# Nine groups of small DMA transfers moved from SyncE's queue to GpSimd's in a fused decoder trunk

## The chip, the cores and the metric

One core of one Trainium2 chip runs the whole program in one launch. The metric is device microseconds (us) of one execution. Lower is better.

Engine names are those of the profile: PE is TensorE (matmul), PEld its weight loads, DVE is VectorE, ACT is ScalarE, POOL is GpSimd, SP is SyncE, which in this kernel only issues transfers. SPq is SP's issuing of a transfer. In the trace each engine works through its own list in the order in which the program wrote it, and idle time ahead of one instruction delays all that stand behind it on that engine.

## What is computed

Two layers of a decoder trunk on 256 tokens of width 1024. A layer is a feed-forward block, a mixing block and a second feed-forward block. The mixing block projects the tokens once and hands the columns to three groups of heads: a depthwise causal convolution of 31 taps, an attention, and a gated DeltaNet. The DeltaNet part is what the change touches. For each of 6 heads and 4 chunks of 64 tokens it needs the inverse of a unit lower triangular matrix:

```python
L = jnp.where(strict, jnp.einsum('bhncd,bhnsd->bhncs', k_beta, k) * decay, 0.0)
eye = jnp.eye(C, dtype=F32)
T = lax.linalg.triangular_solve(eye + L, jnp.broadcast_to(eye, L.shape), left_side=True, lower=True)
u = T @ v_beta
w = T @ (k_beta * jnp.exp(g)[..., None])
```

## The kernel before

The weights come from DRAM in pieces of up to 1 MB into four buffers named `raw`, all issued by SP. ACT rounds each piece to a high part `hi`, DVE makes the rest `lo`, and PE multiplies with three products (hi by hi, hi by lo, lo by hi). A piece's buffer is free again when its last reader is done, and only then may SP issue the next piece into it.

The order of the work on each engine is set while the program is written: a `Clock` object (class at L78, `note` at L133) keeps an estimated time for every engine, and `tick` (L1659) lets a dozen generators (`sides`) add their next instructions when the estimate says that their inputs are ready. All engine calls pass through one helper line, L171, so every row of the profile says L171 and is told apart by its tile's name.

The inverse runs in these steps:

1. `pairs` (L1257) writes the products of all heads into `LD` (a part of the tile shown as `xin_LT`), and four transfers (L1266) bring the 32x32 diagonal blocks to the DRAM tensor `scr_l`.
2. `inverse` (L1367) reads the 16x16 blocks back with two transfers (L1378) into `Lb`, 96 blocks on 96 partitions. POOL makes `Um`, a part of the same buffer, with four multiplications (L1382).
3. DVE does the substitution on all 96 blocks, 15 steps of a product into `T` and a subtraction from `W` (L1385 to L1391), and a copy that turns the result into `W[:, 1]` (L1392).
4. Four transfers (L1398) write `W` to `scr_w`, two for the plain inverse and two for the turned copy, and two transfers (L1400) read it back as 32x32 blocks into `Wc`.
5. POOL clears a tile (`S6a`), and PE joins the blocks to the 64x64 inverses, starting from `Wc` and `Lb`.

`scr_w` is cleared once, after the first feed-forward block: POOL sets a tile `E` to zero and two transfers (L1962) bring it to DRAM.

Beside the inverse runs the convolution of 31 taps (`taps`, L1522; `tap`, L1498). A tap is done in one of two ways: by one DVE instruction, or by a product on ACT into a tile `ctap` followed by an addition on POOL into `cacc` (L1509 and the two lines after it):

```python
m = sb([128, S], "ctap", bufs=2)
act.activation(m, hc[:, b, k:k + S], AF.Copy, scale=w)
gp.tensor_tensor(ca[:, b], ca[:, b], m, op=OP.add)
```

`ctap` has two buffers, so ACT's product number n can start only when POOL's addition number n - 2 is done. While the estimate has DVE busy with the substitution, the taps go this second way.

Also in this stretch PE works on the queries and keys of the attention (`rotary`, L1705): three pairs of projections, each into its own PSUM bank, which ACT copies out (`rope`, L1711; rows COPY Y<-pm), and then on the values (`mv`, L1837), which reuse the banks that these copies have freed.

Of the kernel before, what the change touches and what calls it, by code (L numbers as in the profile page):

```python
# [79 lines left out]
class Clock:  # L80


    def __init__(self):
        self.t = dict(pe=0.0, act=0.0, dve=0.0, gp=0.0, dma=0.0)
        self.writes, self.reads, self.used, self.slots, self.free = {}, {}, {}, {}, {}
        self.table = None
        self.filler = None
# [45 lines left out]
    def note(self, engine, op, args, kw):  # L133
        if op == "preload_act_table_set":
            self.t["act"] += 1.28 if args[0] != self.table else 0.0
            self.table = args[0]
            return
        out = kw.get("out", args[0] if args else None)
        ins = [x for x in list(args[0 if "out" in kw else 1:]) + [v for k, v in kw.items() if k not in ("out", "accum_out")]
               if hasattr(x, "tensor")]  # L140
        name = out.tensor.name
        start = max([self.t[engine], self.free.get(name, 0.0), self.last(self.reads, out), engine != "dma" and self.ready(out)]
                    + [self.ready(x) + 0.1 for x in ins])
        filler = self.filler
        if engine == "dve" and filler:
            self.filler = None
            while start - self.t["dve"] > HOLE and filler():
                pass
            self.filler = filler
            start = max(start, self.t["dve"])  # L150
        if engine == "dma":
            n = self.size(out) * out.shape[0] * 4 / 360e3
            self.t["dma"] = start + n
            end = start + n + (4.5 if "scr_" in name + ins[0].tensor.name else 2.0)
        else:
            end = self.t[engine] = start + self.cost(engine, op, out, ins)
        for log, aps in ((self.writes, [out, kw.get("accum_out", out)]), (self.reads, ins)):
            for x in aps:
                lo, hi = (0, 1 << 40) if engine == "dma" and x is out else self.span(x)
                w = log.setdefault(x.tensor.name, [])  # L160
                w[:] = [y for y in w if not (lo <= y[0] and y[1] <= hi)] + [(lo, hi, end)]
                self.used[x.tensor.name] = max(self.used.get(x.tensor.name, 0.0), end)
# [15 lines left out]
def trunk(ctx, tc, t, out):  # L178
    nc = tc.nc
# [1 line left out]
    psum = ctx.enter_context(tc.tile_pool(name="ps", bufs=1, space=PSUM))  # L181
    ctx.enter_context(tc.manual_schedule())
    clock = Clock()
    act, dve, pe, gp, sp = (clock.engine(n, e) for n, e in (("act", nc.scalar), ("dve", nc.vector), ("pe", nc.tensor),
                                                            ("gp", nc.gpsimd), ("dma", nc.sync)))

    def sb(shape, tag, dt=F32, bufs=1):
        return clock.tile(tag, bufs, pool.tile(shape, dt, name=tag, tag=tag, bufs=bufs))

    def ps(shape, tag, bufs=1):  # L190
        return clock.tile("p" + tag, bufs, psum.tile(shape, F32, name="p" + tag, tag="p" + tag, bufs=bufs))
# [64 lines left out]
    p = ps([128, 128], "x")  # L256
# [367 lines left out]
    def rstd(p=None):  # L624
        r = nscr["r"]
        if p is None:
            p = ps([128, S], "x")
            mm(p, ones, nscr["sq"][:, OB_ORDER[0]], True)
        act.activation(r, p, AF.Ln, bias=eps, scale=1.0 / D)
        act.activation(r, r, AF.Exp, scale=-0.5)  # L630
# [375 lines left out]
    scr_l = nc.dram_tensor("scr_l", [12, 4, 32, 32], F32, kind="Internal").ap()  # L1006
    scr_w = nc.dram_tensor("scr_w", [2, 12, 4, 32, 32], F32, kind="Internal").ap()
    late = {}

    def mixing(l, G, normed, nxt):  # L1010
# [47 lines left out]
        def until(*names):  # L1058
            while any(n not in ev for n in names):
                yield  # L1060
# [78 lines left out]
        LD = LT[:, :NH * 256].rearrange("p (h t x) -> p h t x", t=2, x=128)  # L1139
# [102 lines left out]
        def products(h, rhs):  # L1242
            b, r = half(h)
            yield from room()
            p = pside([128, 384], True)
            mm(p[:, 0:256], kh[r, b, 0:128], rhs[r, b], True)
            mm(p[:, 256:384], kh[r, b, 128:256], rhs[r, b, 128:256], True)
            yield soon(p)
            let_go(p)
            if rhs is kh:  # L1250
                d, e = (x.rearrange("p (a x) -> p a x", x=128)[:, 0:3:2] for x in (p, PT[:, h]))
                dve.tensor_tensor(LD[:, h], d, e, op=OP.mult)
                dve.tensor_tensor(LX[:, h], p[:, 128:256], PT[:, h, 128:256], op=OP.mult)
            else:
                dve.tensor_tensor(PT[:, h], p, PT[:, h], op=OP.mult)

        def pairs():  # L1257
            yield from until("kh")
            for h in range(NH):
                yield from until(("decay", h))  # L1260
                yield (kh, PT[:, h])
                yield from products(h, kh)
            yield (LD,)
            for q in range(4):
                c = slice(32 * q, 32 * q + 32)
                sp.dma_start(out=scr_l.rearrange("g b j i -> b j g i")[q], in_=LD.rearrange("p h t x -> p (h t) x")[c, :, c])  # L1266
            ev["LT"] = True
            yield from until("qh")
            for h in range(NH):
                yield (qh,)  # L1270
                yield from products(h, qh)
            ev["PT"] = True
# [84 lines left out]
        W = sb([96, 2, 16, 16], "W")  # L1357
# [9 lines left out]
        def inverse():  # L1367
# [6 lines left out]
            Lb = buf[0:96, 0:256].rearrange("p (j i) -> p j i", i=16)  # L1374
            Um, X = (buf[:, o:o + 384].rearrange("p (m i) -> p m i", i=32) for o in (256, 640))
            for i in range(2):
                c = slice(16 * i, 16 * i + 16)
                sp.dma_start(out=Lb[48 * i:48 * i + 48], in_=scr_l.rearrange("h b j i -> (h b) j i")[:, c, c])  # L1378
            yield (LD,)
            LM = LD.rearrange("p h t x -> p (h t) x")  # L1380
            for q in QUAD:
# [3 lines left out]
            for j in range(15):  # L1385
                n, ni = j + 1, 15 - j
# [7 lines left out]
            C = sb([128, 2, 12, 32], "Wc")  # L1394
            for f in range(2):
                for i in range(2):
                    c = slice(16 * i, 16 * i + 16)
                    sp.dma_start(out=scr_w[f].rearrange("h b c i -> (h b) c i")[:, c, c], in_=W[48 * i:48 * i + 48, f])  # L1398
            for f in (1, 0):
                sp.dma_start(out=C[:, f], in_=scr_w[f].rearrange("h b c i -> (b c) h i"))  # L1400
            yield from until("kh")
            wide = sb([128, 1536], "S6a")
            TA, X64 = (wide[:, o:o + 768].rearrange("p (m i) -> p m i", i=64) for o in (0, 768))
# [2 lines left out]
            def joined(shape=(12, 32)):  # L1406
                p = pside([128, shape[0] * shape[1]], True)
                return p, p.rearrange("p (m i) -> p m i", i=shape[1])
# [3 lines left out]
            p, o = joined()  # L1412
# [8 lines left out]
            p, o = joined()  # L1421
# [17 lines left out]
            p, o = joined()  # L1439
# [9 lines left out]
            p, o = joined()  # L1449
# [13 lines left out]
            for i in range(2):  # L1463
                yield from room()
                p, o = joined((6, 64))
# [5 lines left out]
            for i in range(2):  # L1471
                yield (XB[:, :, i],)
                yield from room()
                p, o = joined((6, 64))
# [97 lines left out]
        def attention():  # L1572
# [81 lines left out]

        sides.update((s, None) for s in (
            key_norms(), query_norms(), decays(), pairs(), gate_conv(), values_beta(), inverse(), delta_rule(), attention(),
            taps(0), taps(1), convolution()))

# [158 lines left out]
        for i in range(2):  # L1817
            o = bank()
            n = 2 - i
# [81 lines left out]
    for i in range(2):  # L1901
        for j in range(2):
            p = ps([128, 4, 128], f"a{2 * i + j}")
# [33 lines left out]
    for n, (l, ph) in enumerate(order):  # L1937
        nxt = None
        if n + 1 < len(order):
            nl, nph = order[n + 1]  # L1940
            nxt = ((nl, 3 * nph + 1), (nl, 3 * nph))

        def normed(after=(), scaled=False, norm=True, l=l, ph=ph, n=n, G=G):
            if n and norm:
                rstd()
            h = modulate_whole(G["gs"], need_mod(l, 3 * ph), after) if ph == 1 else \
                modulate(G["gs"], need_mod(l, 3 * ph), after, scaled)
            if n == 0:
                cfg["wide"] = ("x", "x")
            cfg["lo_pool"] = True  # L1950
            cfg["mixing"] = ph == 1
            return h

        if ph == 1:
            G = mixing(l, G, normed, nxt)
        else:
            G = ffn(l, 1 if ph == 0 else 2, G, normed, 2 if ph == 0 else 8, nxt)
        if n == 0:
            zero = sb([128, 384], "E", bufs=3)
            gp.memset(zero, 0.0)  # L1960
            for f in range(2):
                sp.dma_start(out=scr_w[f].rearrange("h b c i -> (h b c i)").rearrange("(p n) -> p n", n=384), in_=zero)  # L1962
            dve.tensor_copy(negdb, late["neg"][:, 0])
            dve.tensor_copy(negsb, late["neg"][:, 1])
            dve.tensor_copy(gt, late["neg"][:, 2])
            side_dma.append(load_rows(1))
# [23 lines left out]
```

## Time and profile before

| what | us |
|---|---|
| three runs | 1217.0, 1206.73, 1216.96 |
| their median | 1216.96 |
| the profiled execution | 1213.49 |
| its span, first to last instruction | 1211.7 |
| PE busy, share of the span | 1139.0, 94% |
| DVE busy | 895.1, 74% |
| ACT busy | 621.0, 51% |
| POOL busy | 132.9, 11% |

The mean clock that TensorE was granted is 0.965 of full speed. The two mixing blocks lie about 235 to 415 us and 825 to 1005 us from the start of the span; the steps of the inverse are at 295 to 353 us in the first and at 887 to 942 us in the second. A row of a timeline gives the start, the time until the last instruction of the row ends, the engine, the line, the operation with its tiles, and the count; in brackets stands the time that the engine sat idle before it and what ended that.

### The profile page before, as it was taken

Reading aid. Unit: us, or ns where it says so; the run is one execution under the profiler, and the core shown is the slowest. Engines: PE = TensorE matmul, PEld = TensorE weight load, DVE = VectorE, ACT = ScalarE, POOL = GpSimd, SP = SyncE. Lnnn points to the kernel's source line nnn. Section 1 sums busy time; section 2 is a strip of 40 time slices with the busy share of each in tenths; the row PEclk is TensorE's granted clock in tenths of the full one; section 3 lists DMA queues with packets and bytes.
Section 4 is the critical chain, followed back from the end, with each engine's and each line's share of the span. In section 5 each row is a group of like instructions: output and inputs, shape, how many; then the busy total and the mean of one; then the engine's idle time right before and its main releaser. Section 6 shows DMA issues by size and latency. Waiting matters only on the chain.

```text
span 1211.7 us, 22081 instructions
## 1 busy us (share of the span) xinstructions
PE 1139.0 (94%) x9085; PEld 1060.6 (88%) x9085; DVE 895.1 (74%) x1364; ACT 621.0 (51%) x1061; POOL 132.9 (11%) x139
## 2 busy tenths in 40 slices
PE   5799999999798779999999999999989989999997
PEld 4799999878677779999999999997868779999996
DVE  5778877658886588878769887774879938866554
ACT  4364444447646455444446544444656656544443
POOL 0610000102420010000001000001027101000001
PEclk9899999999879889999999999999988989999999
DMA  8759888656261376979764997893543514786640
GB/s 318 243 197 327 310 297 316 178 169 192 58 205 37 108 240 216 322 262 338 256 229 166 328 323 257 294 295 93 174 149 72 176 56 154 260 262 224 178 155 35
DMA packets 185740, 256.52 MB, mean 212 GB/s; under 512 B 26704, under 2 KB 152744, under 8 KB 185640
## 3 DMA queue, kind: packets, MB, share of 16 engines
q1 hardware_dynamic: 185640, 255.12, 63.1%
q8 instruction: 71, 1.16, 0.4%
q14 instruction: 29, 0.24, 0.1%
HBM read 252.86 MB, written 2.23 MB: 211 GB/s over the span
## 4 chain that ended last, share of the span: by engine, by line
PE 74%; DVE 16%; ACT 6%; issue 2%; POOL 1%; DMA 1%; SPq 0%; POOLq 0%; ACTq 0%; DVEq 0%
PE pm L171 45%; PE pa L171 27%; DVE adaacc L171 3%; DVE lo L171 2%; DVE H L171 2%; PE px L171 2%; ACT hi L171 1%; DVE W L171 1%; DVE v L171 1%; ACT L171 1%; DVE T L171 1%; DVE cacc L171 1%; DVE tmp L171 1%; DVE mod L171 1%; DMA xin_LT<-in_x_dram 1%
## 5 line engine op out<-in xcount | busy, mean ns | idle before, releaser
L171 PE MATMUL pm<-H,hi 128*128 128x256 f32 x2816 | 505.8, 282 | 1.4 <-DVE H L171 1.2
L171 DVE TENSOR_TENSOR lo<-raw,hi 128x1024 fp32r<-128x1024 f32 (+1 forms) x300 | 361.7, 1227 | 109.8 <-ACT hi L171 109.6
L171 PEld LDWEIGHTS pm<-H,hi 128*128 128x128 f32 x2816 | 431.9, 189 | 4.0 <-DVE H L171 2.0
L171 ACT CAST hi<-raw 128x1024 fp32r<-128x1024 f32 (+1 forms) x306 | 312.3, 1042 | 211.0 <-PE pm L171 93.8
L171 PE MATMUL pm<-H,lo 128*128 128x256 f32 x1408 | 392.5, 281 | 1.3 <-DVE lo L171 1.3
L171 PEld LDWEIGHTS pm<-H,lo 128*128 128x128 f32 x1408 | 264.7, 189 | 1.7 <-DVE lo L171 1.7
L171 PE MATMUL pa<-Y,hi 128*128 128x256 f32 x1312 | 245.7, 290 | 11.9 <-ACT S3a L171 7.5
L171 PEld LDWEIGHTS pa<-Y,hi 128*128 128x128 f32 x1312 | 208.3, 196 | 14.8 <-ACT S3a L171 7.9
L171 PE MATMUL pa<-Y,lo 128*128 128x256 f32 x656 | 187.8, 286 | 0.0
L171 PEld LDWEIGHTS pa<-Y,lo 128*128 128x128 f32 x656 | 129.5, 197 | 0.0
L171 ACT CAST Y<-tmp 128x256 fp32r<-128x256 f32 x88 | 35.9, 408 | 131.5 <-DVE tmp L171 131.5
L171 POOL TENSOR_TENSOR xin_LT<-xin_LT 128x256 f32<-128x256 f32 x35 | 27.1, 774 | 648.7 <-ACT xin_LT L171 646.4
L171 DVE SCALAR_TENSOR_TENSOR adaacc<-raw,c_act,adaacc 128x1024 f32<-128x1024 f32 x70 | 93.9, 1342 | 1.6
L171 POOL TENSOR_TENSOR cacc<-cacc,ctap 128x256 f32<-128x256 f32 x68 | 60.5, 890 | 204.8 <-DVE cacc L171 155.8
L171 DVE SCALAR_TENSOR_TENSOR Lb<-raw,c_act,Lb 128x1024 f32<-128x1024 f32 x56 | 71.8, 1283 | 4.3 <-DMA raw<-in_w_ada_dram 3.1
L171 DVE TENSOR_TENSOR Y<-tmp,Y 128x256 fp32r<-128x256 f32 x88 | 37.5, 426 | 41.7 <-ACT Y L171 41.7
L171 PE MATMUL pm<-Y,raw 128*128 128x256 f32 x288 | 66.8, 384 | 0.0
L171 PEld LDWEIGHTS pm<-Y,raw 128*128 128x128 f32 x288 | 53.4, 190 | 8.9 <-issue 1.0
L171 ACT ACTIVATE tmp<-pm 128x256 f32<-128x256 f32 x84 | 31.8, 379 | 52.1 <-PE pm L171 52.0
L171 PE MATMUL pa<-hi,Y 128*128 128x512 f32 x176 | 54.8, 393 | 0.0
L171 DVE TENSOR_REDUCE mod<-px 128x4 f32<-128x512 f32 x34 | 23.4, 689 | 33.6 <-PE px L171 33.5
L171 ACT ACT_TABLE_LOAD x28 | 35.9, 1283 | 14.9 <-DVE v L171 13.8
(301 smaller groups left out, 1337.8 us busy)
## 6 DMA issues: line engine op xcount, KB each, us to landing
raw<-in_w_ada_dram SPq DMA_DIRECT2D x70, 1024.0 KB
raw<-in_ffn_w_gate_dram SPq DMA_DIRECT2D x44, 1024.0 KB
raw<-in_ffn_w_up_dram SPq DMA_DIRECT2D x44, 1024.0 KB
raw<-in_ffn_w_down_dram SPq DMA_DIRECT2D x44, 1024.0 KB
raw<-in_w_in_dram SPq DMA_DIRECT2D x12, 1024.0 KB
raw<-in_w_in_dram SPq DMA_DIRECT2D x20, 512.0 KB
raw<-in_w_out_dram SPq DMA_DIRECT2D x16, 512.0 KB
raw<-in_w_in_dram SPq DMA_DIRECT2D x4, 768.0 KB
```

The lines of the kernel that those rows point to most:

```text
L171: return getattr(real, op)(*args, **kw)
```

## The change

The four groups of transfers of each inverse (to `scr_l`, to `Lb`, to `scr_w`, to `Wc`: twelve transfers a layer) and the two that clear `scr_w` are issued by `nc.gpsimd` instead of `nc.sync`. The planner gets a second DMA time, `dma2`, so that in its estimate these transfers no longer push those of SP. The substitution stays on DVE, and no tile, buffer count or wait of another instruction is written differently.

```diff
@@ class Clock
-        self.t = dict(pe=0.0, act=0.0, dve=0.0, gp=0.0, dma=0.0)
+        self.t = dict(pe=0.0, act=0.0, dve=0.0, gp=0.0, dma=0.0, dma2=0.0)
...
-        if engine == "dma":
+        if engine.startswith("dma"):
             n = self.size(out) * out.shape[0] * 4 / 360e3
-            self.t["dma"] = start + n
+            self.t[engine] = start + n
...
@@ trunk
-    act, dve, pe, gp, sp = (clock.engine(n, e) for n, e in (("act", nc.scalar), ("dve", nc.vector), ("pe", nc.tensor),
-                                                            ("gp", nc.gpsimd), ("dma", nc.sync)))
+    act, dve, pe, gp, sp, qd = (clock.engine(n, e) for n, e in (
+        ("act", nc.scalar), ("dve", nc.vector), ("pe", nc.tensor), ("gp", nc.gpsimd), ("dma", nc.sync), ("dma2", nc.gpsimd)))
...
@@ pairs
-                sp.dma_start(out=scr_l.rearrange("g b j i -> b j g i")[q], in_=LD.rearrange("p h t x -> p (h t) x")[c, :, c])
+                qd.dma_start(out=scr_l.rearrange("g b j i -> b j g i")[q], in_=LD.rearrange("p h t x -> p (h t) x")[c, :, c])
...
@@ inverse
-                sp.dma_start(out=Lb[48 * i:48 * i + 48], in_=scr_l.rearrange("h b j i -> (h b) j i")[:, c, c])
+                qd.dma_start(out=Lb[48 * i:48 * i + 48], in_=scr_l.rearrange("h b j i -> (h b) j i")[:, c, c])
...
-                    sp.dma_start(out=scr_w[f].rearrange("h b c i -> (h b) c i")[:, c, c], in_=W[48 * i:48 * i + 48, f])
+                    qd.dma_start(out=scr_w[f].rearrange("h b c i -> (h b) c i")[:, c, c], in_=W[48 * i:48 * i + 48, f])
             for f in (1, 0):
-                sp.dma_start(out=C[:, f], in_=scr_w[f].rearrange("h b c i -> (b c) h i"))
+                qd.dma_start(out=C[:, f], in_=scr_w[f].rearrange("h b c i -> (b c) h i"))
...
@@ after the first feed-forward block
-                sp.dma_start(out=scr_w[f].rearrange("h b c i -> (h b c i)").rearrange("(p n) -> p n", n=384), in_=zero)
+                qd.dma_start(out=scr_w[f].rearrange("h b c i -> (h b c i)").rearrange("(p n) -> p n", n=384), in_=zero)
```

The lists of PE, DVE and ACT are the same in both programs, row by row. Two lists differ.

On POOL, from the end of the first feed-forward block to the taps beside the first inverse (`xin_LT` in the additions is the scratch of a norm, in the transfers it is `LD`; `E` is the zero tile; `cacc` takes the taps):

```order
 L171 TENSOR_TENSOR xin_LT<-xin_LT 128x256 x7
 L171 MEMSET E 128x384
+L171 DMA scr_w<-E 128x384 x2
 L171 TENSOR_TENSOR cacc<-cacc,ctap 128x256 x4
+L171 DMA scr_l<-xin_LT 32x12x32 x4
+L171 DMA Lb<-scr_l 48x16x16 x2
 L171 TENSOR_TENSOR Lb<-xin_LT,kc 32x384 x4
+L171 DMA scr_w<-W 48x16x16 x4
+L171 DMA Wc<-scr_w 128x12x32 x2
 L171 MEMSET S6a 32x12x32
 L171 TENSOR_TENSOR cacc<-cacc,ctap 128x256 x30
```

Six transfers that wait for the substitution's result, or for each other, now stand ahead of thirty additions of taps. The second layer's rows read the same, without the clearing of `scr_w`.

On SP, at the same place of the first layer (the `raw` rows are pieces of weights):

```order
 L171 DMA raw<-in_w_in_dram 128x8x128
 L171 DMA raw<-in_w_in_dram 128x4x384 x2
-L171 DMA scr_l<-xin_LT 32x12x32 x4
-L171 DMA Lb<-scr_l 48x16x16 x2
-L171 DMA raw<-in_w_ada_dram 128x2x1024
-L171 DMA raw<-in_w_in_dram 128x8x256
-L171 DMA scr_w<-W 48x16x16 x4
-L171 DMA Wc<-scr_w 128x12x32 x2
+L171 DMA raw<-in_w_ada_dram 128x2x1024
+L171 DMA raw<-in_w_in_dram 128x8x256
 L171 DMA raw<-in_w_in_dram 128x8x128
 L171 DMA raw<-in_w_out_dram 128x1024 x8
```

SP's list is now one of weight pieces alone, in the same order as before.

## Rows read from the trace of the kernel before

**Rows 1.** The page, part 1: busy us, share of the span, instructions.

```profile
PE 1139.0 (94%) x9085; PEld 1060.6 (88%) x9085; DVE 895.1 (74%) x1364; ACT 621.0 (51%) x1061; POOL 132.9 (11%) x139
```

**Rows 2.** Waits of SP's queue: us in total, times, longest us.

```profile
SPq L171 <- DVE W L171: 54.9, 2, 27.7
SPq L171 <- POOL E L171: 14.0, 1, 14.0
```

**Rows 3.** Timeline of SP, 215 to 350 us, then 870 to 960 us.

```profile
251.20 0.40 SPq L171 DMA_DIRECT2D raw<-in_w_in_dram  x1
...
328.63 2.07 SPq L171 DMA_DIRECT2D scr_w<-W  x4
332.51 1.14 SPq L171 DMA_DIRECT2D Wc<-scr_w  x2
337.58 0.37 SPq L171 DMA_DIRECT2D raw<-in_w_in_dram  x1
...
920.38 2.06 SPq L171 DMA_DIRECT2D scr_w<-W  x4
924.22 1.15 SPq L171 DMA_DIRECT2D Wc<-scr_w  x2
```

**Rows 4.** Timeline of PE, 326 to 362 us, then 918 to 955 us.

```profile
331.11 0.51 PE L171 MATMUL pm<-hi,H 128*128 128x384 f32 x2
...
335.07 1.64 PE L171 MATMUL pa<-Q,S3a 64*128 64x256 f32 x4 [3.28 <-DVE PT L171]
...
924.42 0.51 PE L171 MATMUL pm<-hi,H 128*128 128x384 f32 x2
...
926.41 0.92 PE L171 MATMUL pa<-Q,S3a 64*128 64x256 f32 x4 [1.31 <-DVE PT L171]
```

**Rows 5.** Timeline of DVE, 303 to 350 us, then 880 to 950 us.

```profile
314.74 0.16 DVE L171 TENSOR_TENSOR T<-W,Lb 96x15 f32<-96x15 f32 x1
...
317.00 0.63 DVE L171 TENSOR_TENSOR T<-W,Lb 96x60 f32<-96x60 f32 x1
...
319.56 0.77 DVE L171 TENSOR_TENSOR T<-W,Lb 96x64 f32<-96x64 f32 x1
...
906.97 0.16 DVE L171 TENSOR_TENSOR T<-W,Lb 96x15 f32<-96x15 f32 x1
...
909.74 0.22 DVE L171 TENSOR_TENSOR T<-W,Lb 96x63 f32<-96x63 f32 x1
```

**Rows 6.** Timeline of POOL, 286 to 350 us, then 880 to 950 us.

```profile
298.25 4.62 POOL L171 TENSOR_TENSOR Lb<-xin_LT,kc 32x384 f32<-32x384 f32 x4
302.93 0.41 POOL L171 MEMSET S6a<- 32x384 f32 x1
316.76 0.79 POOL L171 TENSOR_TENSOR cacc<-cacc,ctap 128x256 f32<-128x256 f32 x1 [13.43 <-DVE T L171]
...
909.75 0.79 POOL L171 TENSOR_TENSOR cacc<-cacc,ctap 128x256 f32<-128x256 f32 x1 [14.20 <-DVE W L171]
```

**Rows 7.** Timeline of ACT, 303 to 350 us, then 880 to 950 us.

```profile
316.12 0.51 ACT L171 ACTIVATE ctap<-hc,colB 128x256 f32<-128x256 f32 x1
...
317.25 0.91 ACT L171 ACTIVATE ctap<-hc,colB 128x256 f32<-128x256 f32 x2
...
325.34 0.59 ACT L171 COPY Y<-pm 128x512 f32<-128x512 f32 x1 [0.22 <-PE pm L171]
...
918.44 0.59 ACT L171 COPY Y<-pm 128x512 f32<-128x512 f32 x1 [0.47 <-PE pm L171]
```

**Rows 8.** Groups of POOL instructions by line: busy us, mean ns of one, idle before.

```profile
L171 POOL TENSOR_TENSOR xin_LT<-xin_LT 128x256 f32<-128x256 f32 x35 | 27.1, 774 | 648.7 <-ACT xin_LT L171 646.4
```

**Rows 9.** Stretches: length, busy us (instructions) by engine, granted TensorE clock, DMA share, GB/s.

```profile
335.00:351.50 16.50, 16.43 (x47) 12.98 (x48) 16.33 (x28) 6.93 (x11) 6.39 (x8) 0.50 0.46 131
...
926.40:928.70 2.30, 2.29 (x12) 1.71 (x13) 2.30 (x4) 1.97 (x5) 2.06 (x4) 1.00 0.67 91
928.70:938.80 10.10, 10.10 (x30) 7.83 (x29) 9.96 (x19) 4.87 (x8) 5.98 (x6) 0.50 0.48 147
```

More of the change, by code (lines that the diff above doesn't have):

```diff
@@ L141, in note @@
         name = out.tensor.name
-        start = max([self.t[engine], self.free.get(name, 0.0), self.last(self.reads, out), engine != "dma" and self.ready(out)]
+        start = max([self.t[engine], self.free.get(name, 0.0), self.last(self.reads, out), not engine.startswith("dma") and self.ready(out)]
                     + [self.ready(x) + 0.1 for x in ins])
@@ L158, in note @@
             for x in aps:
-                lo, hi = (0, 1 << 40) if engine == "dma" and x is out else self.span(x)
+                lo, hi = (0, 1 << 40) if engine.startswith("dma") and x is out else self.span(x)
                 w = log.setdefault(x.tensor.name, [])
```

## The prediction

> **What bounds the kernel now.** Start with the page: PE is busy for 94% of the span [rows 1], so an edit away from PE changes the time only where PE stands still, or is made to. The waits of SP's queue come next, because the change empties it. SP waited 54.9 us in two waits for W, the substitution's result, and 14.0 us once for POOL's zero tile [rows 2]. That looks like much to win. Then the SP timeline: after the read-back of Wc at 332.51, SP's next piece of weights goes out only at 337.58, with 3.9 us of further waiting between [rows 3]; in the program it waits for DVE to finish the low part of an earlier piece. The hold for W had nothing behind it that was ready. So the time at stake is not SP's. The PE timeline shows the little that is: in the first layer PE stands 3.28 us before 335.07, in the second 1.31 us before 926.41, both on DVE, which is late with `PT` because it has just done the substitution [rows 4].
>
> **What goes.** The wait for W on SP: worth 0, by the rows just read. The 14.0 us wait for the zero tile: behind it stand a 96 KB constant and a piece for the modulation sums; the next projection piece goes out at 251.20 [rows 3], and it waits for PE to free its buffer. Worth 0, covered by that wait. Without this cover it could give at most the 14.0 us, which I leave out, since PE has no wait on a transfer there.
>
> **What comes, at one place per layer.** On POOL the four writes of `scr_w` wait for W, the two reads of `Wc` wait for those writes, and thirty additions of taps stand behind them, with the clearing of `S6a` ahead. Before, the first of these additions ran at 316.76 and at 909.75, while DVE was still substituting [rows 6]. Who waits for POOL: ACT's tap products, which have two buffers. ACT did one at 316.12 and two more from 317.25 [rows 7]; after the change it stops at the third. Behind that stop, in ACT's list, come eight more products and then the copy of the second query-key bank, which ran at 325.34 [rows 7]. Who waits for ACT: PE, whose value products at 331.11 [rows 4] write into the bank that this copy frees. The chain POOL, ACT, PE is where the price is paid.
>
> **When POOL starts its hold.** A counter-effect comes first. The substitution has 30 operations on DVE. Until POOL's additions start, they are quick: ten from 314.74 to 317.00, twelve from 906.97 to 909.74, that is 0.23 us each. Beside POOL's additions one takes 0.63 or 0.77 us, where the 96x63 in the second layer took 0.22 [rows 5]. After the change POOL stands still meanwhile, so 30 operations take about 7.0 us (30 x 0.23) instead of 13.9 (to the first write at 328.63 [rows 3]) and 13.4. W is ready at 321.8 and 914.0. This helps DVE by almost 7 us, so PE's two stalls on DVE go.
>
> **How long POOL is held.** From W: six issues (call their sum s), the landing of the writes, the clearing. On SP the writes took 2.07 us, and the reads started 1.81 us after these were issued (332.51 - 330.70; second layer 1.78) [rows 3]. The clearing takes 0.41 us [rows 6]. The trace shows no transfer issued by POOL, so s is bounded. From below: SP's own, 2.07 + 1.14 = 3.2 us [rows 3]. From above: let POOL make each piece of a transfer at its pace in an addition, 774 ns for 256 elements, 3.0 ns for one [rows 8]. A write has 48x16 = 768 runs, 2.3 us; a read 128x12 = 1536, 4.6 us; s = 4 x 2.3 + 2 x 4.6 = 18.6 us. I take s = 8.0, about as many times the lower end as it is below the upper one. It is near six times POOL's own small operation on 32x384, 4.62 / 4 = 1.16 us [rows 6], with a little more for the two longer reads. Below nothing is excluded: an issue takes POOL some time.
>
> The Trainium skill (DMA: Bandwidth & Descriptors, section Specifications) gives about 1 us to the first byte for a GpSimd transfer and 0.6 for one of SP; as an estimate by that page s is 6 x 1.0 = 6 us. No trace here shows it yet, and the sum does not use it.
>
> **The sum.** First layer: 321.8 + 8.0 + 1.81 + 0.41 = 332.0, first addition. Before, the copy of the bank ended 9.17 us after the first addition (325.34 + 0.59 - 316.76 [rows 6, 7]), and the ping-pong between ACT and POOL in between is unchanged. So it ends at 341.2, and the products of 331.11 start then. They took 0.68 us until the stall (335.07 - 3.28 - 331.11). PE is at 341.9 where it was at 335.07: +6.8 us. Second layer: 914.0 + 8.0 + 1.78 + 0.41 = 924.2; the copy ended 9.28 us after the first addition; 933.5; with 0.68, 934.2 against 926.41: +7.7 us. Later work of ACT and DVE (the casts of the value and gate weights, the low parts) moves by no more than PE does, because PE frees the buffers they fill.
>
> The clock adds something. After the first layer's stall TensorE was granted 0.50, its 1.2 GHz level, from 335.0 to 351.5; in the second layer, with its shorter stall, it kept 2.4 GHz until 928.7 and had 0.50 until 938.8 [rows 9]. PE will now stand 8 to 10 us in both. For the second layer I add 1.5 us, between 0 and 2.9: the 2.3 us that ran at the high level at most double, and 0.6 us is allowed for a later rise. Both ends count.
>
> The reads of `Lb` also move to POOL, from 298.25 on, after the additions [rows 6]. They must have landed by 314.74. With two landings of 1.8 us that leaves 12.9 us for six issues, so with 8.0 it costs nothing, and it begins to cost only if the issues pass 12.9 us.
>
> Total: 6.8 + 7.7 + 1.5 = 16.0 us, or 2 x s in general, since the other terms cancel. The profiled execution took 1213.49 us, so 1229.5, forecast 1230 us. The median of the runs shown, 1216.96, lies 3.5 us higher, their lowest 6.8 lower.
>
> **The rivals.**
> Cheap issues, within 1%: if POOL issues as fast as SP (s = 3.2), the sum is 2.0 + 2.9 and 0 to 1.5 for the clock, 5 to 6.4 us: 1219. For it: nothing in these transfers but their small runs asks more of POOL than of SP. Against: POOL's small operations take 1.16 us. The border of +1% (12.1 us) is at s = 6.1.
> No effect: the waiting transfers don't hold the additions behind them, so POOL adds taps beside the substitution as before, and nothing on PE's path moves: 1213. Against it: on SP the same wait held the queue 27.7 us [rows 2].
> By the Trainium skill (the same page, section Issuing engines are not separate DMA queues) initiating on several engines saves only the sequencer's issue time, which is usually small. By that rule alone this change would be such a case, 1213; the rows agree that SP's time is worth nothing, but the rule leaves out what POOL has behind the wait.
> Faster: POOL's hold ends before ACT's stop reaches PE, and DVE's 7 us are kept. The copy would have to end by 331.1, so the first addition by 321.9: W must be ready earlier still, or ACT be let past. Then both stalls go, 3.28 + 1.31 = 4.6 us, and the clock may stay up: half of 16.5 and of 10.1 us at 0.50 [rows 9], up to 13.3. That is 1196 to 1209, say 1203. Against it: W at 321.8 leaves no time for six issues and a landing.
> Much slower: s beyond 18.6 us, or issues that pass 12.9 us ahead of the substitution, which then shifts too: over 1252.
>
> **How the numbers follow.** The forecast's own case, s from 6.1 to 18.6, has 0.54: it gives 12 to 38.6 us (with 2.9 for the clock), 1226 to 1252. Much slower 0.08, cheap issues 0.18, no effect 0.12, faster 0.08. So slower by over 1% is 0.62, within 1% 0.30, faster 0.08; one per cent is about what a measurement of this kernel can tell from no change. The range runs from 1212, which takes in no effect and cheap issues, to 1252, the upper bound of the issues. About 0.16 to 0.18 is left out.
>
> **What would show it.** Right: POOL's first addition of the thirty at about 332 and 924; substitution operations at 0.2 us throughout, W at about 322; a wait of ACT's third product on POOL of 14 us or so; PE's stall at the first value products for ACT's copy, 9 to 10 us, and none on `PT`; SP without waits for W and no piece of weights earlier that PE had waited for. Wrong: additions of taps between the transfers and W's end on POOL; substitution operations of 0.77 us still; PE standing at `PT` as before; or issues on POOL near 0.5 us.

## The result and the profile after

The changed kernel took 1225.43 us (median of 13 runs, 1219.41 to 1231.92), the kernel before 1213.48 us in the same comparison (13 runs, 1206.73 to 1218.73). The ratio is 1.0093, 95% interval 1.0066 to 1.0119: slower by nearly 1%. The forecast was 1230, range 1212 to 1252. The total came out near it; two of its terms were too large and one was much too small, as will be seen.

The profiled execution took 1227.08 us, its span is 1225.3 us, 13.6 longer than that of before, at a mean granted clock of 0.952 instead of 0.965. Part 1 of its page answers to [rows 1]; the second line is ACT's group of tap products, with its idle time at the end:

```profile
PE 1144.8 (93%) x9085; PEld 1064.6 (87%) x9085; DVE 884.5 (72%) x1364; ACT 620.4 (51%) x1061; POOL 156.1 (13%) x165
...
L171 ACT ACTIVATE ctap<-hc,colB 128x256 f32<-128x256 f32 x68 | 33.9, 508 | 49.0 <-POOL cacc L171 49.0
```

PE's busy time rose by 5.8 us although it does the same 9085 products; keep that for the clock, below. ACT now stands 49 us in front of tap products, for POOL.

The chain of the forecast is read engine by engine. First POOL's timeline in both layers, which answers to [rows 6] and, for the transfers, to [rows 3]:

```profile
298.04 2.48 POOL L171 DMA_DIRECT2D scr_l<-xin_LT  x4
303.67 1.46 POOL L171 DMA_DIRECT2D Lb<-scr_l  x2 [3.15 <-PE pm L171]
305.14 4.42 POOL L171 TENSOR_TENSOR Lb<-xin_LT,kc 32x384 f32<-32x384 f32 x4
318.97 2.92 POOL L171 DMA_DIRECT2D scr_w<-W  x4 [9.41 <-DVE W L171]
324.48 2.07 POOL L171 DMA_DIRECT2D Wc<-scr_w  x2 [2.58 <-DMA scr_w<-W]
...
327.07 6.35 POOL L171 TENSOR_TENSOR cacc<-cacc,ctap 128x256 f32<-128x256 f32 x8
...
911.41 2.92 POOL L171 DMA_DIRECT2D scr_w<-W  x4 [8.68 <-DVE W L171]
917.37 2.06 POOL L171 DMA_DIRECT2D Wc<-scr_w  x2 [3.03 <-issue]
...
919.96 6.33 POOL L171 TENSOR_TENSOR cacc<-cacc,ctap 128x256 f32<-128x256 f32 x8
```

POOL waits for W, writes, waits for the writes, reads, clears, and only then adds taps: at 327.07 and 919.96, where before it began at 316.76 and 909.75. The six issues cost 2.92 + 2.07 = 4.99 us (4.98 in the second layer).

ACT's timeline answers to [rows 7]: the second product of the stretch, the third, and the copy of the bank.

```profile
313.46 0.51 ACT L171 ACTIVATE ctap<-hc,colB 128x256 f32<-128x256 f32 x1
327.83 0.51 ACT L171 ACTIVATE ctap<-hc,colB 128x256 f32<-128x256 f32 x1 [13.87 <-POOL cacc L171]
...
335.26 0.57 ACT L171 COPY Y<-pm 128x512 f32<-128x512 f32 x1
...
920.71 0.51 ACT L171 ACTIVATE ctap<-hc,colB 128x256 f32<-128x256 f32 x1 [15.82 <-POOL cacc L171]
...
928.14 0.57 ACT L171 COPY Y<-pm 128x512 f32<-128x512 f32 x1
```

Two buffers, two products, then a stop of 14 and 16 us; the copy, which was at 325.34 and 918.44, is late by 9.9 and 9.7 us. PE's timeline answers to [rows 4]; the last two rows are two later places of the second layer.

```profile
306.67 0.90 PE L171 MATMUL pa<-kc,v 128*128 128x128 f32 x3 [2.01 <-ACT v L171]
...
335.88 1.01 PE L171 MATMUL pm<-hi,H 128*128 128x384 f32 x2 [8.08 <-ACT Y L171]
337.14 1.65 PE L171 MATMUL pa<-Q,S3a 64*128 64x256 f32 x4
...
928.76 1.01 PE L171 MATMUL pm<-hi,H 128*128 128x384 f32 x2 [10.55 <-ACT Y L171]
930.01 1.65 PE L171 MATMUL pa<-Q,S3a 64*128 64x256 f32 x4
...
971.92 2.53 PE L171 MATMUL pa<-S6a,xin_LT 64*64 64x64 f32 x24 [0.91 <-DVE xin_LT L171]
...
998.14 0.79 PE L171 MATMUL pa<-Y,hi 128*128 128x256 f32 x2 [3.08 <-ACT S3a L171]
```

PE stands 8.08 and 10.55 us for ACT's copy, and no longer for `PT`. At `pa<-Q,S3a` it is 2.07 us behind before (337.14 against 335.07) and 3.60 us (930.01 against 926.41). That is far less than the stalls, because PE came to them early, by 3.3 us in the first layer and 6.2 in the second, and because its waits for `PT` are gone. For comparison, the same PE places in the trace of before:

```profile
310.10 0.90 PE L171 MATMUL pa<-kc,v 128*128 128x128 f32 x3 [4.90 <-ACT v L171]
...
966.20 1.58 PE L171 MATMUL pa<-S6a,xin_LT 64*64 64x64 f32 x24 [0.38 <-DVE xin_LT L171]
...
984.30 0.80 PE L171 MATMUL pa<-Y,hi 128*128 128x256 f32 x2 [3.77 <-ACT S3a L171]
```

The wait for ACT's `v` fell from 4.90 to 2.01 us, and to 2.00 in the second layer. The reason stands in DVE's timeline, of before:

```profile
295.54 7.61 DVE L171 TENSOR_TENSOR H<-Y,H 128x256 fp32r<-128x256 f32 x8
```

and of after (the low parts of the tokens, six taps, the first step of the substitution, the turned copy behind it):

```profile
295.36 4.36 DVE L171 TENSOR_TENSOR H<-Y,H 128x256 fp32r<-128x256 f32 x8
...
304.32 5.53 DVE L171 SCALAR_TENSOR_TENSOR cacc<-hc,colB,cacc 128x256 f32<-128x256 f32 x6
...
311.61 0.17 DVE L171 TENSOR_TENSOR T<-W,Lb 96x15 f32<-96x15 f32 x1
...
318.70 0.38 DVE L171 COPY W<-W 96x256 f32<-96x256 f32 x1
```

Before, POOL made `Um` from 298.25 on [rows 6], beside these eight low parts. Now the waiting reads of `Lb` hold `Um` until 305.14, and the low parts take 3.25 us less. `Um` slows six taps of DVE instead (5.53 us, 2.95 before), close to where DVE had waited 2.1 us for ACT.

In the second layer the shorter wait gave PE 2.8 us more. These are the windows from that wait to just before the value products, for before and then for after: length, busy us of PE, PEld, DVE, ACT, POOL with their instructions, then the granted clock, the DMA share and GB/s.

```profile
902.30:923.90 21.60, 21.57 (x136) 19.18 (x137) 18.41 (x44) 15.61 (x29) 11.91 (x15) 0.86 0.10 10
```

```profile
898.70:917.50 18.80, 18.80 (x135) 17.04 (x136) 16.97 (x49) 6.12 (x11) 6.86 (x9) 1.00 0.13 14
```

Behind the wait of 4.90 us TensorE ran for a part of the window at its 1.2 GHz level, behind the wait of 2.00 us it did not. In the first layer of the same execution the clock was at 0.51 for 3.5 us behind the wait of 2.01 us too, so the length of the wait alone doesn't decide it.

The rest of the loss is not at the stall. In the second layer PE's delay is 3.60 us at 930.01, 5.72 at 971.92 (966.20 before) and 13.84 at 998.14 (984.30 before). Between the last two places the windows show, for before and then for after:

```profile
966.20:984.30 18.10, 12.90 (x120) 10.98 (x120) 7.70 (x18) 12.86 (x30) 2.30 (x2) 0.97 0.00 1
```

```profile
971.90:998.10 26.20, 23.14 (x120) 19.44 (x120) 7.86 (x18) 12.30 (x30) 2.29 (x2) 0.51 0.00 1
```

The same 120 products took 23.14 us of PE instead of 12.90, at a granted clock of 0.51, that is at the 1.2 GHz level, instead of 0.97. So 8.1 of the 13.6 us are lost 40 us after the stall, with no longer wait in between. Whether this belongs to the change had to be asked of a second execution.

### The profile page after: what moved, and what is told of

Same layout as the page of the kernel before. It is cut to its first block, busy times and chain, and to the rows that moved or that the text cites. A ratio compares the mean times of both kernels' runs of the same rounds, so it can differ in the third digit from the quotient of the medians.

```text
span 1225.3 us, 22097 instructions
## 1 busy us (share of the span) xinstructions
PE 1144.8 (93%) x9085; PEld 1064.6 (87%) x9085; DVE 884.5 (72%) x1364; ACT 620.4 (51%) x1061; POOL 156.1 (13%) x165
## 4 chain that ended last, share of the span: by engine, by line
PE 73%; DVE 15%; ACT 6%; POOL 2%; issue 2%; DMA 1%; SPq 0%; POOLq 0%; DVEq 0%; ACTq 0%
PE pm L171 44%; PE pa L171 27%; DVE adaacc L171 3%; DVE lo L171 2%; PE px L171 2%; DVE cacc L171 2%; ACT hi L171 1%; DVE H L171 1%; POOL cacc L171 1%; DVE v L171 1%; ACT L171 1%; DVE mod L171 1%; DVE tmp L171 1%; DVE Lb L171 1%; DMA xin_LT<-in_x_dram 1%
## 5 line engine op out<-in xcount | busy, mean ns | idle before, releaser
L171 PE MATMUL pa<-Y,hi 128*128 128x256 f32 x1312 | 246.7, 291 | 11.9 <-ACT S3a L171 6.9
L171 POOL TENSOR_TENSOR cacc<-cacc,ctap 128x256 f32<-128x256 f32 x68 | 64.8, 953 | 158.1 <-DVE cacc L171 151.3
L171 ACT ACTIVATE ctap<-hc,colB 128x256 f32<-128x256 f32 x68 | 33.9, 508 | 49.0 <-POOL cacc L171 49.0
```

The costliest lines, as they stand in the source:

```text
L171: return getattr(real, op)(*args, **kw)
```

## The experiments

There are three theories. The first is that of the prediction: transfers that wait for W hold POOL's additions, these hold ACT, and ACT holds PE. The second: transfers issued by POOL are slow in themselves, wherever they stand. The third: the loss comes from SP's changed list. None of the kernels leaves work out.

**First run: the writes back on SP.**

```diff
-                    qd.dma_start(out=scr_w[f]..., in_=W[48 * i:48 * i + 48, f])
+                    sp.dma_start(out=scr_w[f]..., in_=W[48 * i:48 * i + 48, f])
...
-                qd.dma_start(out=C[:, f], ...)
+                sp.dma_start(out=C[:, f], ...)
```

> Only the four writes of scr_w from W and the two reads of Wc go back to SP; the transfers to scr_l and Lb and the clearing stay on POOL. Theory 1 (the hold: six transfers that wait for W stand ahead of thirty additions on POOL, ACT stops for want of ctap, PE stops for ACT's copy): PE has no wait of 8 us or more for ACT's Y, the additions run beside the substitution again and stretch it to about 13 us, and the time is 1207 to 1214 us, no slower than before. Theory 2 (transfers that POOL issues are slow in themselves, and each group pays its share): half of the moved transfers are still on POOL, so half of the loss of 12 us stays, 1219. Theory 3 (the loss comes from SP's list, which brings the weight pieces at other times): SP's list is that of before from scr_w on, 1213, but PE's wait for ACT's Y would have gone in this case too; what tells it from theory 1 is the next run.

Measured 1219.55 us, before 1216.04 in this comparison, ratio 1.0021 (0.9990 to 1.0053): no loss clear of noise is left, and nothing is won. The first theory had expected 1207 to 1214, which was missed. ACT's copy holds PE nowhere. Half of the loss, as the second theory wants it, would be about 1.005, just inside the interval; the second run decides there. The low parts are quick (4.37 us), so PE came to the stretch 2.8 us earlier than before and 5 us in the second layer. It did not keep that: with additions beside it again the substitution has steps of 0.78 us, and PE waits for DVE instead. DVE's timeline, one step, and PE's two waits, of which the second comes from the low parts of weights that stand behind the substitution:

```profile
319.22 0.78 DVE L171 TENSOR_TENSOR T<-W,Lb 96x64 f32<-96x64 f32 x1
```

```profile
334.01 1.65 PE L171 MATMUL pa<-Q,S3a 64*128 64x256 f32 x4 [3.70 <-DVE PT L171]
...
924.42 0.69 PE L171 MATMUL pm<-lo,H 128*128 128x384 f32 x1 [5.08 <-DVE lo L171]
```

**Second run: only the writes of `scr_w` and the reads of `Wc` on POOL** (the other transfers are `sp.dma_start` again).

> Only the four writes of scr_w from W and the two reads of Wc are on POOL; scr_l, Lb and the clearing are on SP as before. Theory 1: the whole loss is here. Um runs at 298 again, the low parts H take 7.6 us again, so the substitution starts near 314.7, W is ready near 321.8, the first addition follows 8.4 us later as in the changed kernel, near 330, and PE waits 10 us or more for ACT's Y in both layers: 1225 to 1231. Theory 2: six of twelve transfers, half of the loss, 1219. Theory 3: SP's list is that of before up to the second projection piece, so most of the loss goes, 1213 to 1217.

Measured 1228.62 us, ratio 1.0096 (1.0063 to 1.0129): the whole loss with half of the transfers. The second theory, by which each group pays its share, falls. The third is not yet out, since SP's list is that of before only up to W's transfers; the third run, which has the changed kernel's list of SP row by row, and the fifth settle it. POOL's timeline and PE's longest wait (us in total, times, longest):

```profile
297.29 4.64 POOL L171 TENSOR_TENSOR Lb<-xin_LT,kc 32x384 f32<-32x384 f32 x4
321.17 3.09 POOL L171 DMA_DIRECT2D scr_w<-W  x4 [19.24 <-DVE W L171]
...
329.31 6.35 POOL L171 TENSOR_TENSOR cacc<-cacc,ctap 128x256 f32<-128x256 f32 x8
```

```profile
PE pm L171 <- ACT Y L171: 8.2, 1, 8.2
```

`Um` is early again, W 2.2 us later than in the changed kernel, and the first addition stands where it was expected. PE waits 8.2 us for the copy in the first layer and 6.6 in the second, not the 10 or more expected: it comes later to the place, by 2.9 us more of wait for ACT's `v` in each layer.

**Third run: the taps planned behind the hold.** All transfers stay on POOL; the planner is told that POOL is busy until such a transfer has been issued.

```diff
             self.t[engine] = start + n
+            if engine == "dma2":
+                self.t["gp"] = max(self.t["gp"], start + 0.8)
```

> All transfers stay on POOL as in the changed kernel; the planner's time of POOL is moved to the end of each transfer that POOL issues, so taps by way of ACT and POOL are not planned while POOL is held, and ACT's copies of the query-key banks stand ahead of the products into ctap. Eleven taps fewer per layer go by way of ACT and POOL, DVE does them. Theory 1: PE has neither the wait for ACT's Y nor the one for PT, the substitution keeps its 7 us, and the time is 1204 to 1211, faster than both kernels. Theory 2 and theory 3: nothing in the transfers or in SP's list has changed, so the loss stays, 1222 to 1228.

Measured 1192.8 us, ratio 0.9827 (0.9768 to 0.9886), better than expected. In ACT's list the two last copies of query-key banks and four casts now stand ahead of the stretch's first product into `ctap`. The new plan changes more than this order: eleven taps of each layer go to DVE instead of ACT and POOL, some copies out of PSUM change places between ACT and DVE, and PE's two waits of 3.8 us for ACT's `S3a` in before are gone. ACT's timeline (the two added lines make the helper's line L173), POOL's, and a window of the stretch with the clock as its third number from the end:

```profile
325.27 0.59 ACT L173 COPY Y<-pm 128x512 f32<-128x512 f32 x1 [3.60 <-PE pm L173]
325.75 0.91 ACT L173 ACTIVATE ctap<-hc,colB 128x256 f32<-128x256 f32 x2
```

```profile
318.79 2.92 POOL L173 DMA_DIRECT2D scr_w<-W  x4 [9.07 <-DVE W L173]
...
326.89 6.96 POOL L173 TENSOR_TENSOR cacc<-cacc,ctap 128x256 f32<-128x256 f32 x6
```

```profile
300.00:352.00 52.00, 47.84 (x565) 41.81 (x563) 49.72 (x105) 29.12 (x57) 30.78 (x30) 1.00 0.50 146
```

POOL is held just as long, W to first addition 8.1 us, and nobody waits for it. PE does 565 products in this window and keeps 2.4 GHz in this execution. POOL's transfers and SP's list are those of the changed kernel, and the loss is gone. The new plan could hide one, but the fifth run, the same plan with the transfers on SP, is slower and not faster; so the second and the third theory fall. That the same hold costs nothing when no work that PE needs stands behind it is shown more closely by the eighth and tenth run.

**Fourth run: sixteen writes instead of four.**

```diff
-                    qd.dma_start(out=scr_w[f]...[:, c, c], in_=W[48 * i:48 * i + 48, f])
+                    for r in range(0, 48, 12):
+                        qd.dma_start(out=scr_w[f]...[r:r + 12, c, c], in_=W[48 * i + r:48 * i + r + 12, f])
```

> The changed kernel with each of the four writes of scr_w cut in four by partitions: sixteen issues, the same bytes. Theory 1: twelve more issues of 0.5 to 0.7 us each stand ahead of the additions, 6 to 8.5 us per layer, and the time grows by about twice that, to 1237 to 1242. Theory 2, if it is the bytes or their runs that cost, and theory 3: the same bytes and the same list of SP, 1225 to 1228.

Measured 1238.95 us, ratio 1.0166 (1.0133 to 1.0199). POOL's timeline and PE's wait:

```profile
320.17 9.49 POOL L171 DMA_DIRECT2D scr_w<-W  x16 [9.41 <-DVE W L171]
331.62 2.08 POOL L171 DMA_DIRECT2D Wc<-scr_w  x2 [1.96 <-DMA scr_w<-W]
...
334.24 6.34 POOL L171 TENSOR_TENSOR cacc<-cacc,ctap 128x256 f32<-128x256 f32 x8
```

```profile
PE pm L171 <- ACT Y L171: 15.7, 1, 15.7
```

From W to the first addition it takes 14.07 us instead of 8.10. Twice that difference is 11.9 us; the ratios differ by 0.0073, 9 us, with some 5 of uncertainty. The rule "two us for one us of issue" fits within that.

**Fifth run: the third run's order with every transfer on SP** (`("dma2", nc.sync)` in place of `("dma2", nc.gpsimd)`; the "fourteen groups" of the expectation are the nine of the title).

> The order of PE, DVE and ACT of the third run (products into ctap behind ACT's copies), with all fourteen groups of transfers issued by SP again. Theory 1 (what counts is which work stands behind a wait; the queue itself is worth nothing once no tap is behind it): PE has no wait for ACT's Y or for PT here either, the substitution keeps its 7 us since no addition runs beside it, and the time is within 1% of the third run, 1190 to 1205; Um runs early again, so the low parts H take 7.6 us and up to 3 us per layer come back. Theory 2 (transfers that POOL issues cost by themselves): 5 us or more per layer below the third run, under 1185. A third reading, that the gain of the third run needs POOL's queue free of SP's weight pieces: 1206 or more.

Measured 1205.66 us, ratio 0.9953 (0.9922 to 0.9984): 1.3% above the third run, a little outside what the first theory gave and at the edge of the third reading (1206 or more). Additions don't run beside the substitution here either (W's steps take 7.1 us, POOL is idle from 304.1 to 332.2), and PE waits for neither `Y` nor `PT`. SP's list is row by row that of before. So the third run's plan by itself is worth about half a per cent; how much of that is the order of the taps and how much the waits for `S3a`, 7.5 us in before and gone here too, was not separated. The rest of the third run's gain needs something that its transfers on POOL do.

**Sixth run: the same order, only the writes and the reads of `Wc` on SP.**

> The third run's order of PE, DVE and ACT, the four writes of scr_w from W and the two reads of Wc on SP, the transfers to scr_l and Lb and the clearing on POOL. Um stays behind Lb's issue, so the low parts H take 4.4 us and the substitution starts early; Wc is read back 1.5 to 3 us sooner than in the third run. Theory 1: PE did not wait for Wc in the third run, so this gives within 0.5% of it, and up to 6 us less than the run with all on SP: 1187 to 1198. Theory 2: the six transfers cost by themselves, 1180 to 1187.

Measured 1198.85 us, ratio 0.9890 (0.9852 to 0.9928). It gains about half of that rest, which points to the transfers to `scr_l` and `Lb`, the only ones that it has on POOL beside the clearing.

**Seventh run: the changed kernel once more.**

> The changed kernel once more, for TensorE's clock from 970 to 1003 us. If the stretch at 0.50 there is part of the price of the stall, it is there again; if it comes and goes from execution to execution with the same stalls, it is absent here, and the span is 5 to 8 us shorter than 1225.3.

Median 1224.34 us, ratio 1.0091 (1.0060 to 1.0122). Its profiled execution has stalls of like size (9.7 and 10.1 us for ACT's `Y`) and a span of 1217.6 us, 7.7 shorter. PE's timeline at the two later places, and the window between them:

```profile
970.73 1.58 PE L171 MATMUL pa<-S6a,xin_LT 64*64 64x64 f32 x24 [0.91 <-DVE xin_LT L171]
...
990.36 0.80 PE L171 MATMUL pa<-Y,hi 128*128 128x256 f32 x2 [3.76 <-ACT S3a L171]
```

```profile
970.70:990.40 19.70, 14.34 (x121) 12.12 (x121) 7.77 (x18) 12.38 (x30) 2.30 (x2) 0.87 0.00 1
```

At the first place PE is 4.5 us behind before, at the second 6.1, at the end 5.9. So of the 13.6 us between the first two profiles 5.9 were there in both executions, and 7.7 only where the clock stayed at the 1.2 GHz level. The medians, 9 to 12 us apart, lie between. The first experiment's profile, in which PE never waited for ACT's copy, has the same stretch for the same products:

```profile
970.00:996.20 26.20, 23.13 (x120) 19.45 (x120) 7.86 (x18) 12.32 (x30) 2.29 (x2) 0.51 0.00 1
```

The second and the fourth run, in which PE did wait for the copy, did these products at 0.88 and 1.00. So this stretch comes and goes and doesn't follow from the stall. The mean granted clock of the 13 runs of after was 0.950 to 0.962, with the longest spans at the lowest clock; the runs of before beside the first four experiments had 0.956 to 0.971. The changed kernel thus runs at a somewhat lower clock, but in which stretches the runs without a profile lost it isn't known.

**Eighth, ninth and tenth run**, on one chip with the same runs of before: the third run's kernel again; the same with only the transfers to `scr_l` and `Lb` on SP; the sixth run's kernel again.

> The third run's kernel again with more rounds, beside the next two on one chip. Its time is again below both kernels, 1190 to 1200, a ratio of 0.980 to 0.988 to the kernel before.

> The third run's order, with the transfers to scr_l and Lb back on SP and the rest on POOL, so that nothing holds POOL ahead of Um. If Um's place is what shortened the low parts H: Um runs near 298, the eight low parts take 7.6 us instead of 4.4, PE's wait for ACT's v is 4.9 instead of 2.0 us in both layers, and the time is 4 to 8 us above the run beside it. If the earlier substitution came from the transfers themselves (Lb sooner in place by way of POOL): the low parts take 4.4 us here too and the time is the same within 2 us.

> The sixth run's kernel again beside the third's. If POOL's queue is worth nothing in this order: within 0.3% of the run of all on POOL. If the additions' start behind Wc on POOL (326.9 against 328.0, and memset after it) or the clock make the difference that the first pair showed: 4 to 8 us slower again.

Measured 1195.83 us, ratio 0.9849 (0.9809 to 0.9888); 1208.06 us, ratio 0.9949 (0.9920 to 0.9978); 1198.22 us, ratio 0.9854 (0.9810 to 0.9898). Eighth and tenth are equal within noise: with nothing behind the wait that PE needs, it doesn't show which engine issues the writes. The ninth is 1% slower, more than the 4 to 8 us expected. DVE's low parts and PE's wait for ACT's `v` in the first layer, of the eighth:

```profile
295.07 4.36 DVE L173 TENSOR_TENSOR H<-Y,H 128x256 fp32r<-128x256 f32 x8
```

```profile
PE pa L173 <- ACT v L173: 2.0, 1, 2.0
```

and of the ninth:

```profile
295.17 7.62 DVE L173 TENSOR_TENSOR H<-Y,H 128x256 fp32r<-128x256 f32 x8
```

```profile
PE pa L173 <- ACT v L173: 4.9, 1, 4.9
```

The two programs differ only in who issues these six transfers of a layer, and so in where `Um` runs; the lists of PE, DVE and ACT are the same. The profiled spans differ by 13.0 us, and the waits for `v` make 5.8 of them. The clock makes most of the rest. Behind the second layer's wait it fell in the ninth run and not in the eighth, as between before and after (2.3 us). And the ninth's profile has this window, with PE busy throughout at the 1.2 GHz level; in the eighth's the clock is down there only for shorter pieces, and the same products take 4.0 us less:

```profile
945.00:972.00 27.00, 27.00 (x243) 21.68 (x241) 16.50 (x43) 13.55 (x39) 2.17 (x3) 0.50 0.13 40
```

The fifth run's profile, with `Um` early as well, has such a stretch from 949 to 976 us, and the third, sixth and tenth have none there; that `Um`'s place brings it is not shown by one profile of each. The expectation's other reading, `Lb` sooner in place by way of POOL, falls with the 7.62 us. That the profit is `Um`'s place, and not the queue's, is shown as far as `Um`, the low parts and the wait move together in every run; a kernel with `Um` moved by itself, in the same order of the rest, was not run.

The kernel of the third and eighth run beats both kernels of this document, by 1.5 to 1.7% against the one before.

## Why the prediction was right, and where not

The step of the prediction that failed in size is the issue time s, and with it the delay of the two stalls; the step that it missed is what POOL's own late work does to DVE; and the clock was looked for in the wrong place.

1. *What goes is worth 0* (the waits of SP): right. SP no longer waits for W, and no wait of PE on a transfer went with it.
2. *The chain POOL, ACT, PE*: right in each link. ACT stopped at its third product for 13.87 and 15.82 us (about 14 was given), PE for 8.08 and 10.55 us (9 to 10), and not for `PT`. The first run shows it by removal, the second with these six transfers alone, the third by order and the fourth by size. The rival "no effect" falls with them.
3. *The substitution without additions beside it takes 7.0 us*: measured 7.06 (318.67 less 311.61). *W ready at 321.8 and 914.0*: 318.97 and 911.41, because the step started earlier. This was missed: the prediction counted the reads of `Lb` on POOL as covered or harmful ("costs nothing") and didn't ask what `Um`, queued behind them, would stop disturbing. It gave 2.9 us of PE's wait for `v` in each layer, and in the second another 2.8 us, because the clock stayed up behind the shorter wait.
4. *The issues, s = 8.0*: mis-sized, 4.99 us, within its bounds of 3.2 and 18.6. POOL's pace per element, from [rows 8], doesn't apply to runs: a write of 768 runs took 0.73 us. The border that the prediction put at s = 6.1 was not reached, so by its own sum, 2s, this should have been 10 us. The measured +0.93% lies just inside the group "within 1%", to which the prediction gave 0.30 and not its 0.62. *Landing 1.8*: 2.59 and 3.04. The Trainium skill (DMA: Bandwidth & Descriptors, section Specifications) gives about 1 us to the first byte for POOL; the estimate of 6 us made from it lay nearer than the value taken. That figure is of the first byte, though, and what is summed here is the time for which POOL was busy issuing, 0.73 to 1.03 us for each of the six.
5. *First addition at 332.0 and 924.2*: 327.07 and 919.96. *PE +6.8 and +7.7*: +2.07 and +3.60 us. The additions came 4.9 and 4.2 us earlier than forecast and PE 4.7 and 4.1, so behind the first addition the chain was sized rightly. By the start of the second inverse the first layer's 2 us had been made up: DVE's low parts began at 887.39, against 887.76 before.
6. *The clock, +1.5*: the term that failed the other way. Of the 13.6 us of the profiled pair, 10.2 come behind `pa<-Q,S3a` of the second layer (3.60 to 13.84), most of it in stretches at the 1.2 GHz level. The prediction looked for the clock only next to the stall. Since the first experiment's profile has the stretch from 970 to 996 us without the stall, 7.7 of these us are not shown to be a price of the change.

So the sign came from the right mechanism. That the total lay so near is luck: 16.0 us was the sum of stalls taken too large by 9 us (14.5 against 5.7) and a clock taken too small by up to 9. What both executions of the changed kernel show is 5.9 us; where the rest of the 9 to 12 us between the medians lies is open. So is what decides whether TensorE stays at 1.2 GHz from 972 to 998 us: the two executions of the changed kernel reach that place with nearly the same waits.

## What to carry to other kernels

Before a waiting transfer goes onto an engine that also computes, list what stands behind it there and who needs that, and tell the planner too: with the copies behind the hold the kernel lost 9 to 12 us, and once they stood ahead the hold cost nothing that can be measured here. A queue change moves every later instruction of that engine, so look also for work that it takes out of another engine's way: here it made the larger part of the fastest kernel's gain. Where PE stalls, compare two executions before giving all the time that follows to the change.

## What the runs showed of the hardware that was not expected

- A transfer issued by POOL cost 0.59 us with 192 runs (9.49 / 16), 0.62 with 384 (2.48 / 4), 0.73 with 768 (2.92 / 4) and 1.03 with 1536 (2.07 / 2); on SP the last two were 0.52 and 0.57 [rows 3]. Eight times the runs cost 1.75 times the issue, so the number of transfers matters more than that of their runs.
- DVE is slowed beside POOL: eight low parts took 4.36 us alone and 7.62 beside `Um`, six taps 2.95 and 5.53, and a step of the substitution 0.22 and 0.78 beside an addition. The Trainium skill (GPSIMD Engine Reference, section 1. Specifications) says that POOL shares its SBUF interfaces with VectorE and contends with instructions that have two SBUF inputs or run in a 2-port performance mode; these rows, of instructions with two inputs, agree with it. The copy of W, with one input, was slowed too, from 0.38 to 0.82 us in the first experiment; in which mode it ran no trace shows.
- The same 120 products took 12.90 us of PE's time in one execution and 23.14 in another, at 0.97 and 0.51 granted. In the ninth run the profile shows PE at the 1.2 GHz level while it is busy without a gap, 27.00 of 27.00 us at 0.50.
- In the second layer the clock behind the wait for `v` went with the length of the wait in all twelve profiles: 0.86 or 0.87 behind 4.9 us (before, second, fifth and ninth run), 1.00 behind 2.0 us (the other eight).
